# Projections whose high weight tile multiplies both parts of the activations in one product

## The chip, the core and the metric
The kernel runs on one core of a Trainium2 chip. The metric is the device time of one execution in microseconds: 2598.18 us as the median of three runs before the change. PE is TensorE, PEld its weight loads, DVE VectorE, ACT ScalarE, POOL GpSimd, SP SyncE, which issues the DMAs.

## The reference
256 tokens of 2048 features go through two layers of attention and then a block with an S5 state space mixer and an MLP; everything is modulated by vectors that come from large vector-matrix products. What matters here is that most of the arithmetic is dense projections `h @ W` of 256 tokens by 2048 rows of a float32 weight: query, key, value, gate and output projections, a GLU, and the MLP

```python
def sq_relu_mlp(h, w1, w2):
    return jnp.square(jax.nn.relu(h @ w1)) @ w2
```

All of it has to come out in float32 accuracy.

## The kernel before
A weight matrix is cut into column tiles of 128 columns by 2048 rows, 320 tiles in all, in a fixed list (`stream_init`). A tile is loaded in two halves of 128 x 1024 (SP's queue, tag `raw`, four buffers). `_split` (L118) makes two fp32r parts of each half: ScalarE casts the high part `wh` (L130), VectorE (or GpSimd) subtracts it from the raw half and leaves the low part `wl` (L131). High and low parts have five buffers each (tags H and L). Before each tile's products `weights()` makes sure that two more tiles are split ahead (`ahead = 2`) and takes one step of the side jobs: `bg()` loads a chunk of a vector product and adds the chunk before, on VectorE (L210) or on TensorE (L195), by the policy of the stage.

The activations are split in the same way into `aH` and `aL`, each `[128, 16, 256]` (`pair`, `affine_split` L392, L393). `mm_t` (L149) makes 128 output columns by 256 tokens of the next tile: 16 steps over the rows, each with three products of 256 columns,

```python
self.nc.tensor.matmul(ps, h, aH, start=kt == order[0], stop=False)   # L156
self.nc.tensor.matmul(ps, h, aL, start=False, stop=False)            # L157
self.nc.tensor.matmul(ps, l, aH, start=False, stop=kt == order[-1])  # L158
```

Each product loads its own 128 x 128 weight tile. The sum `pj` lies in PSUM in one of four banks (`NPJ = 4`). 288 tiles go through `mm_t`: 48 in layer 0's input projections and 16 in its output, 16 keys, 32 of layer 1's query and gate and 16 of its output, 32 of the GLU and 128 of the MLP. The 32 tiles of the values go through `mm_n` (L173 to L175), where the activations are the loaded operand; it is not changed.

Who reads `pj`: ScalarE copies it (keys, first quarter of the MLP's output L1588), scales it (queries; out_norm's gate, L1037), or takes tanh of it, whereupon VectorE reads it a second time (gates, GLU L1516); in the MLP ScalarE applies Relu (L1579), VectorE squares (L1581), and the square is split again; the later quarters of the MLP's output are added by VectorE (L1590). Where a projection ends a stage (out_norm, GLU, MLP) sums over its output follow on TensorE (`band`) and a chain of small VectorE instructions before the next stage starts.

The order of the instructions on each engine is made by the tile framework's scheduler from the program; each engine runs its queue in order. The forget gate's products (L1109 to L1111) use the same format with a weight tile of 16 columns; the attention's scores (L875) are float32, in two passes each.

Of the kernel before, what the change touches and what calls it, by code (L numbers as in the profile page):

```python
# [101 lines left out]
def bc(ap, n):  # L102
    """ap [p, m] seen as [p, m, n], each element repeated n times."""
    return bass.AP(tensor=ap.tensor, offset=ap.offset, ap=[list(d) for d in ap.ap] + [[0, n]])


class K:
# [11 lines left out]
    def _split(self, eng=None):  # L119
# [4 lines left out]
        for i in range(2):  # L124
            raw = self.raw.tile([128, 1024], F32, name=f"w{j}_{i}", tag="raw")
            nc.sync.dma_start(raw, self.items[j][:, i * 1024:i * 1024 + 1024])
            h = self.hl.tile([128, 8, 128], F32R, name=f"wh{j}_{i}", tag="H")
            l = self.hl.tile([128, 8, 128], F32R, name=f"wl{j}_{i}", tag="L")
# [20 lines left out]
    def mm_t(self, a, order=range(KT)):  # L149
        """[128 columns, 256 tokens] of the next column tile; a[kt] = both parts of [128, 256]."""  # L150
        H, L = self.weights()
        ps = self.pj.tile([128, T], F32, name="pj", tag="pj")
        for kt in order:
            h, l = H[kt // 8][:, kt % 8], L[kt // 8][:, kt % 8]
            aH, aL = a(kt)
            self.nc.tensor.matmul(ps, h, aH, start=kt == order[0], stop=False)  # L156
            self.nc.tensor.matmul(ps, h, aL, start=False, stop=False)  # L157
            self.nc.tensor.matmul(ps, l, aH, start=False, stop=kt == order[-1])  # L158
        return ps

    def mm_n(self, a, half):
        """[128 tokens, 2, 256 columns]: half 0 opens the sum with the first 8 kt, half 1 closes it."""
# [92 lines left out]
    def bg_add(self, *jobs):  # L255
        """Queue (name, generator): the first halves of all, then the second."""
# [4 lines left out]
    def policy(self, engines, split):  # L261
        """The engines that add the chunks, and which halves of the weights GpSimd splits."""
# [3 lines left out]
    def bg(self, n=1, eng=None):  # L266
        """n steps of the vector products: each loads a chunk and adds the one before."""
# [25 lines left out]
    def rsqrt(self, v):  # L293
        """v[128, n] (positive) -> v ** -0.5: a guess from the exponent, a step of Newton's and one of Halley's."""
# [5 lines left out]
        # y = 3/8 of the better guess  # L300
# [9 lines left out]
    def spread(self, col, name="rb"):  # L310
        """col[128 tokens, n, 2] -> PSUM [128, n, 256], the value of each token in every partition."""
# [11 lines left out]
    def colsum(self, ps, src, first, last, cols=None):  # L323
        """ps[128 tokens, 2, n] += src[128, 256].T @ cols[128, n] (cols: ones)."""
# [6 lines left out]
    def bands(self, name):  # L331
        """PSUM [128, 256] of zeros for band()."""
# [7 lines left out]
    def band(self, g, q, cols, src):  # L340
        """Rows 32 q .. of g += cols[128, n].T @ src[128, 256]."""
# [3 lines left out]
    def band_sums(self, g, sel, name):  # L345
        """PSUM [128 tokens, 2, n]: the rows of g that sel[128, n] picks and adds."""
# [20 lines left out]
    def small_bg(self, out, a, b, c, d):  # L367
        """a * (1 + b) and c * (1 + b) + d (without c: d), by halves."""
# [16 lines left out]
    def affine_split(self, src, S, B, dst, js=range(KT)):  # L385
        """dst(kt) = both parts of src(kt) * S + B."""
# [13 lines left out]
    def s5_exp(self, x, t, em1=False):  # L400
        """x, t: lists of [128, 128] scratch; returns exp(x) (or exp(x) - 1) in t[0]."""
# [19 lines left out]
    def cmul(self, o, a, b, t):  # L421
        """complex pairs: o = a * b; t: four scratch tiles."""
# [12 lines left out]
    def s5_compact(self):  # L435
# [25 lines left out]
        # w = (lambda_bar - 1) / a  # L461
# [15 lines left out]
        # powers  # L477
# [5 lines left out]
        # factors of the tables by half blocks: [hb, table (W, V), ri, 8 groups, 4 tokens]  # L483
# [17 lines left out]
        # chunk decay and its squarings, per group ((re, im), (-im, re))  # L501
# [12 lines left out]
    def s5_prod(self, t, xr, xi, lr, li, part):  # L514
        """t = the two products of part 0 (real) or 1 (imaginary) of x * l, x [128, n, 16], l [128, n, 4]."""
# [58 lines left out]
        # C A^|lag| of 4 groups by lag -3 .. 3, zero where the lag is the other direction's  # L574
# [79 lines left out]
    def chunk_inputs(self, w, Ub, q, evac):  # L654
        """w[128 (s, tau, h), 4, 2, 128 (dir, state)], Ub[128, 8, 2, 64], group pairs 4q .. 4q+3:
# [428 lines left out]
    def layer1(self):  # L1084
# [138 lines left out]
        for h in range(16):  # L1223
# [6 lines left out]
            if h:  # L1230
                pv(h - 1)
# [473 lines left out]
```

## Time and profile before

| | before |
|---|---|
| median of 3 runs (lowest, highest) | 2598.18 us (2596.72, 2598.43) |
| profiled execution: span, first to last instruction | 2600.7 us |
| instructions | 52283 |
| granted TensorE clock, mean | 0.946 |
| read from and written to HBM | 613.71 MB, 25.69 MB |

The profile is of one execution; its own time is known by its span alone. A share is the busy time of an engine over the span. Products are pipelined, so the duration of one is longer than the distance to the next; the pace is read from the starts. A granted clock of 1.00 is 2.4 GHz.

### The profile page before, as it was taken

To read this page: it belongs to the slowest core of one execution; us is meant where nothing else is said; L and a number is where in the kernel's file an instruction comes from. 1 tells how busy PE (TensorE), PEld (TensorE's weight loads), DVE (VectorE), ACT (ScalarE), POOL (GpSimd) and SP (SyncE) were. 2 spreads that over 40 slices of the span, in tenths; PEclk is the share of its full clock that TensorE was granted. 3 is DMA by queue.
4 is the path that set the end of the run, shared out by engine and by line. 5 is a ranking of instruction groups with operands and counts; after the bars stand their busy time and mean duration, and the time that the engine had idled before them with its cause. 6 is when DMAs were issued, how large, how long until landed. Compare 5 with 4: busy or idle time off the path is not lost.

```text
span 2600.7 us, 52283 instructions
## 1 busy us (share of the span) xinstructions
PE 2397.3 (92%) x20998; PEld 2172.4 (84%) x20998; DVE 1755.7 (68%) x3223; ACT 1255.6 (48%) x2178; POOL 209.7 (8%) x432
## 2 busy tenths in 40 slices
PE   5699999999899999999997445999899999999997
PEld 1299999999688888898886335998899999999996
DVE  3287878868766555788778998876754554555554
ACT  1455544444365565766555155544544443443442
POOL 0000000000011110000000853000000000000000
PEclk9699999999899999999998766999899999999998
DMA  9999999878779998788776543996355555555552
GB/s 330 343 337 318 333 329 329 317 253 326 252 248 339 333 328 289 264 279 283 258 232 204 182 165 120 331 318 238 119 184 183 184 184 182 186 180 186 182 179 94
DMA packets 203332, 644.92 MB, mean 248 GB/s; under 512 B 41009, under 2 KB 49457, under 8 KB 202705
## 3 DMA queue, kind: packets, MB, share of 16 engines
q1 hardware_dynamic: 195616, 620.47, 69.3%
q0 software_dynamic: 7472, 21.11, 2.1%
q8 instruction: 164, 2.69, 0.4%
q14 instruction: 80, 0.65, 0.1%
HBM read 613.71 MB, written 25.69 MB: 246 GB/s over the span
## 4 chain that ended last, share of the span: by engine, by line
PE 83%; DVE 10%; DMA 3%; ACT 3%; issue 1%; SPq 0%; DVEq 0%; POOL 0%; ACTq 0%
PE pj L156 22%; PE pj L157 21%; PE pj L158 21%; PE g L195 3%; DVE scan_t L1381 3%; PE pjv L173 3%; PE pjv L174 2%; DMA graw<-in_w_mod 2%; PE pjv L175 2%; DVE scan_t L1380 2%; DVE S L1382 2%; PE inc L665 1%; PE st L343 1%; PE kps L617 1%; PE ys L343 1%
## 5 line engine op out<-in xcount | busy, mean ns | idle before, releaser
L131 DVE TENSOR_TENSOR wl<-w,wh 128x1024 fp32r<-128x1024 f32 x638 | 777.6, 1224 | 533.7 <-ACT wh L130 526.0
L130 ACT CAST wh<-w 128x1024 fp32r<-128x1024 f32 x640 | 664.9, 1048 | 717.2 <-PE pj L157 414.0
L157 PE MATMUL pj<-h2L,wh 128*128 128x256 f32 x1024 | 291.1, 286 | 0.4 <-DVE h2L L393 0.3
L156 PE MATMUL pj<-h2H,wh 128*128 128x256 f32 x1024 | 286.8, 286 | 4.7 <-ACT h2H L392 3.6
L158 PE MATMUL pj<-h2H,wl 128*128 128x256 f32 x1024 | 290.7, 285 | 0.0
L156 PE MATMUL pj<-dH,wh 128*128 128x256 f32 x1024 | 290.1, 284 | 0.0
L157 PE MATMUL pj<-dL,wh 128*128 128x256 f32 x1024 | 289.9, 283 | 0.0
L158 PE MATMUL pj<-dH,wl 128*128 128x256 f32 x1024 | 289.9, 283 | 0.0
L210 DVE SCALAR_TENSOR_TENSOR gacc<-graw,csilu,gacc 128x1024 f32<-128x1024 f32 x207 | 264.7, 1279 | 26.0 <-DMA graw<-in_w_mod 16.5
L156 PE MATMUL pj<-hH,wh 128*128 128x256 f32 x768 | 221.5, 289 | 5.2 <-ACT hH L392 4.0
L158 PE MATMUL pj<-hH,wl 128*128 128x256 f32 x768 | 221.4, 289 | 0.5 <-DVE wl L131 0.5
L157 PE MATMUL pj<-hL,wh 128*128 128x256 f32 x768 | 221.1, 288 | 0.0
L195 PE MATMUL g<-graw,czc 128*32 128x256 f32 x1776 | 169.8, 466 | 51.3 <-DMA graw<-in_w_mod 49.9
L156 PEld LDWEIGHTS pj<-h2H,wh 128*128 128x128 f32 x1024 | 196.0, 194 | 5.7 <-ACT h2H L392 4.1
L157 PEld LDWEIGHTS pj<-h2L,wh 128*128 128x128 f32 x1024 | 198.6, 194 | 1.2 <-DVE h2L L393 1.2
L158 PEld LDWEIGHTS pj<-h2H,wl 128*128 128x128 f32 x1024 | 198.8, 194 | 0.1
L156 PEld LDWEIGHTS pj<-dH,wh 128*128 128x128 f32 x1024 | 196.8, 192 | 1.7 <-issue 1.7
L158 PEld LDWEIGHTS pj<-dH,wl 128*128 128x128 f32 x1024 | 196.8, 192 | 0.0
L157 PEld LDWEIGHTS pj<-dL,wh 128*128 128x128 f32 x1024 | 196.8, 192 | 0.0
L195 PEld LDWEIGHTS g<-graw,czc 128*32 128x32 f32 x1776 | 47.2, 120 | 130.5 <-DMA graw<-in_w_mod 105.5
L156 PEld LDWEIGHTS pj<-hH,wh 128*128 128x128 f32 x768 | 148.7, 194 | 8.8 <-ACT hH L392 4.1
L158 PEld LDWEIGHTS pj<-hH,wl 128*128 128x128 f32 x768 | 148.4, 193 | 4.5 <-issue 3.7
(476 smaller groups left out, 5907.6 us busy)
## 6 DMA issues: line engine op xcount, KB each, us to landing
graw<-in_w_mod SPq DMA_DIRECT2D x384, 512.0 KB, 5.7
w<-in_mlp_in SPq DMA_DIRECT2D x128, 512.0 KB, 3.5
w<-in_mlp_out SPq DMA_DIRECT2D x128, 512.0 KB, 3.6
w<-in_a_in SPq DMA_DIRECT2D x96, 512.0 KB, 5.9
graw<-in_w_kvmod SPq DMA_DIRECT2D x64, 512.0 KB, 6.0
w<-in_b_in SPq DMA_DIRECT2D x64, 512.0 KB, 5.8
w<-in_glu SPq DMA_DIRECT2D x64, 512.0 KB, 5.4
w<-in_a_v SPq DMA_DIRECT2D x32, 512.0 KB, 5.8
```

The source lines that it names most:

```text
L130: nc.scalar.copy(h, src)
L131: (eng or (nc.gpsimd if next(self.spl) else nc.vector)).tensor_sub(l, src, h)
L156: self.nc.tensor.matmul(ps, h, aH, start=kt == order[0], stop=False)
L157: self.nc.tensor.matmul(ps, h, aL, start=False, stop=False)
L158: self.nc.tensor.matmul(ps, l, aH, start=False, stop=kt == order[-1])
L173: self.nc.tensor.matmul(ps[:, i], aH[:, s], h, start=half == 0 and i == 0 and k == 0, stop=False)
L174: self.nc.tensor.matmul(ps[:, i], aH[:, s], l, start=False, stop=False)
L175: self.nc.tensor.matmul(ps[:, i], aL[:, s], h, start=False, stop=half == 1 and i == 1 and k == 7)
L195: nc.tensor.matmul(st["g"][32 * q:32 * q + 32], self.cz[c][:, ch * 2 + s], raw[s][:, q * 256:q * 256 + 256], start=st["n"] == 0, stop=ch = ...
L210: nc.vector.scalar_tensor_tensor(acc, raw[s], cc, acc, op0=MUL, op1=ADD)
L343: self.nc.tensor.matmul(g[32 * q:32 * q + n], cols, src, start=False, stop=False)
L1381: e.tensor_add(u, t[:, :, 0], s[:, :, :, c + 1])
```

## The change
`mm_t` takes a whole PSUM bank, `[128, 2, 256]`. Both parts of an activation lie next to each other, so that the high weight tile multiplies both in one product of 512 columns; the product of the low weight tile with `aH` goes to the first half. `total` then adds the two halves: ScalarE copies (or scales) the second half to SBUF, VectorE adds the first half from PSUM. The last three quarters of the MLP's output are added to the accumulator by two VectorE additions. The MLP's Relu becomes a maximum inside the square. Weight parts share one tile (tag HL, five buffers), `pair`, `oo`, `kv` and the S5 stage's buffers are laid out to match, and two `issue_after` orders behind a ScalarE copy are gone.

```diff
-            h = self.hl.tile([128, 8, 128], F32R, name=f"wh{j}_{i}", tag="H")
-            l = self.hl.tile([128, 8, 128], F32R, name=f"wl{j}_{i}", tag="L")
+            hl = self.hl.tile([128, 2, 8, 128], F32R, name=f"w{j}_{i}", tag="HL")
+            h, l = hl[:, 0], hl[:, 1]
...
-        ps = self.pj.tile([128, T], F32, name="pj", tag="pj")
+        ps = self.pj.tile([128, 2, T], F32, name="pj", tag="pj")
         for kt in order:
             h, l = H[kt // 8][:, kt % 8], L[kt // 8][:, kt % 8]
-            aH, aL = a(kt)
-            self.nc.tensor.matmul(ps, h, aH, start=kt == order[0], stop=False)
-            self.nc.tensor.matmul(ps, h, aL, start=False, stop=False)
-            self.nc.tensor.matmul(ps, l, aH, start=False, stop=kt == order[-1])
+            aH, _ = a(kt)
+            self.nc.tensor.matmul(ps, h, view(aH, 0, [[T, 2], [1, T]]), start=kt == order[0], stop=False)
+            self.nc.tensor.matmul(ps[:, 0], l, aH, start=False, stop=kt == order[-1])
         return ps
 
+    def total(self, ps, out=None, scale=1.0):
+        out = self.tmp("pt") if out is None else out
+        t = self.tmp("ps")
+        if isinstance(scale, float) and scale == 1.0:
+            self.nc.scalar.copy(t, ps[:, 1])
+            self.nc.vector.tensor_add(out, ps[:, 0], t)
+        else:
+            self.nc.scalar.mul(t, ps[:, 1], scale)
+            self.nc.vector.scalar_tensor_tensor(out, ps[:, 0], scale, t, op0=MUL, op1=ADD)
+        return out
...
     def pair(self, name):
-        H, L = self.act_tile(F32R, name + "H"), self.act_tile(F32R, name + "L")
-        return lambda kt: (H[:, kt], L[:, kt])
+        t = [self.act.tile([128, 8, 2, T], F32R, name=f"{name}{i}", tag="act") for i in range(2)]
+        return lambda kt: (t[kt // 8][:, kt % 8, 0], t[kt // 8][:, kt % 8, 1])
...
-                nc.scalar.copy(kT[:, i], ps)
+                self.total(ps, kT[:, i])
...
-                ps = self.mm_t(h_)
+                ps = self.total(self.mm_t(h_))
                 t = self.tmp("tg")
                 nc.scalar.activation(t, ps, AF.Tanh, scale=0.5)
...
-            nc.scalar.mul(yg, ps, gate[:, j:j + 1])
+            self.total(ps, yg, gate[:, j:j + 1])
...
-            with self.tc.issue_after(nc.scalar.copy(af, pa).ins):
-                nc.scalar.activation(x[:, j], x[:, j], AF.Identity, scale=V("lg1")[:, j:j + 1],
-                                     bias=V("lb1")[:, j:j + 1])
+            af = self.total(pa)
+            nc.scalar.activation(x[:, j], x[:, j], AF.Identity, scale=V("lg1")[:, j:j + 1],
+                                 bias=V("lb1")[:, j:j + 1])
...
-                ps = self.mm_t(h_)
-                r = self.tmp("r")
-                nc.scalar.activation(r, ps, AF.Relu)
+                r = self.total(self.mm_t(h_))
                 f = self.tmp("r2")
-                v.tensor_mul(f, r, r)
+                v.scalar_tensor_tensor(f, r, 0.0, r, op0=MAX, op1=MUL)
...
-                    nc.scalar.copy(acc[:, j], ps)
+                    self.total(ps, acc[:, j])
                 else:
-                    v.tensor_add(acc[:, j], acc[:, j], ps)
+                    for i in range(2):
+                        v.tensor_add(acc[:, j], acc[:, j], ps[:, i])
```

## Rows read from the trace of the kernel before

**Rows 1.** The page's busy times (share of the span) and instructions of each engine.
```profile
PE 2397.3 (92%) x20998; PEld 2172.4 (84%) x20998; DVE 1755.7 (68%) x3223; ACT 1255.6 (48%) x2178; POOL 209.7 (8%) x432
```
**Rows 2.** The page's chain that ended last, shares of the span by engine and line.
```profile
PE 83%; DVE 10%; DMA 3%; ACT 3%; issue 1%; SPq 0%; DVEq 0%; POOL 0%; ACTq 0%
PE pj L156 22%; PE pj L157 21%; PE pj L158 21%; PE g L195 3%; DVE scan_t L1381 3%; PE pjv L173 3%; PE pjv L174 2%; DMA graw<-in_w_mod 2%; PE pjv L175 2%; DVE scan_t L1380 2%; DVE S L1382 2%; PE inc L665 1%; PE st L343 1%; PE kps L617 1%; PE ys L343 1%
```
**Rows 3.** Busy time by stage; then granted clock, DMA share and GB/s.
```profile
0.00:153.00 153.00, 101.95 (x768) 47.83 (x769) 57.09 (x188) 55.20 (x131) 5.56 (x21) 0.81 0.92 330
153.00:640.00 487.00, 487.00 (x4141) 464.81 (x4141) 393.65 (x606) 240.55 (x413) 22.24 (x45) 1.00 0.90 320
640.00:750.00 110.00, 96.65 (x654) 76.67 (x653) 82.82 (x137) 51.02 (x96) 4.86 (x15) 0.84 0.70 228
750.00:1000.00 250.00, 250.00 (x2566) 217.51 (x2566) 146.24 (x212) 145.11 (x280) 42.52 (x92) 1.00 0.94 328
1000.00:1245.00 245.00, 244.26 (x2123) 218.00 (x2122) 191.99 (x333) 160.37 (x329) 4.84 (x10) 1.00 0.81 278
1245.00:1345.00 100.00, 98.00 (x856) 86.12 (x854) 77.25 (x138) 54.84 (x98) 1.56 (x5) 0.98 0.74 252
1345.00:1620.00 275.00, 167.46 (x2089) 132.00 (x2089) 249.17 (x911) 122.55 (x230) 121.97 (x236) 0.73 0.51 169
1620.00:1815.00 195.00, 195.00 (x1597) 180.58 (x1596) 143.02 (x141) 97.54 (x156) 5.81 (x9) 1.00 0.85 299
1850.00:2575.00 725.00, 724.41 (x6036) 721.76 (x6035) 371.49 (x438) 311.13 (x417) 0.00 (x0) 1.00 0.54 178
```
**Rows 4.** Waits of PE over the span: total us, times, longest us.
```profile
PE g L195 <- DMA graw<-in_w_mod: 49.9, 58, 5.5
...
PE pj L156 <- ACT wh L130: 2.9, 4, 1.2
...
PE pj L158 <- DVE wl L131: 2.0, 3, 1.2
```
**Rows 5.** Timeline of PE in the MLP, start and duration, first and 27th product.
```profile
1999.83 0.28 PE L156 MATMUL pj<-dH,wh 128*128 128x256 f32 x1
...
2002.95 0.28 PE L158 MATMUL pj<-dH,wl 128*128 128x256 f32 x1
```
**Rows 6.** Timeline of PE at the forget gate, first and last of 45 products.
```profile
737.01 0.28 PE L1109 MATMUL zf<-kH,wzH 128*16 128x256 f32 x1
...
742.09 0.28 PE L1111 MATMUL zf<-kH,wzL 128*16 128x256 f32 x1
```
**Rows 7.** Timeline of PE at a head's scores in layer 0, four passes merged.
```profile
167.98 1.03 PE L875 MATMUL sc<-attn_ws 128*128 128x256 f32 x4
168.66 0.47 PE L157 MATMUL pj<-hL,wh 128*128 128x256 f32 x1
```
**Rows 8.** Groups of PE by form: the scores' passes of 256 columns (busy us, mean ns).
```profile
L875 PE MATMUL sc<-attn_ws 128*128 128x256 f32 x32 | 8.3, 379 | 0.0
```
**Rows 9.** Groups of VectorE and ScalarE instructions that read `pj`, and the MLP's square.
```profile
L1590 DVE TENSOR_TENSOR acc<-acc,pj 128x256 f32<-128x256 f32 x47 | 19.8, 421 | 41.3 <-PE pj L158 41.3
L1588 ACT COPY acc<-pj 128x256 f32<-128x256 f32 x16 | 5.8, 365 | 0.0
L1037 ACT ACTIVATE yg<-pj,m 128x256 f32<-128x256 f32 x12 | 5.7, 471 | 1.9 <-PE pj L158 1.9
L1581 DVE TENSOR_TENSOR r<-r 128x256 f32<-128x256 f32 x64 | 26.9, 420 | 0.0
```
**Rows 10.** The page's groups: the two instructions that split a weight half.
```profile
L131 DVE TENSOR_TENSOR wl<-w,wh 128x1024 fp32r<-128x1024 f32 x638 | 777.6, 1224 | 533.7 <-ACT wh L130 526.0
L130 ACT CAST wh<-w 128x1024 fp32r<-128x1024 f32 x640 | 664.9, 1048 | 717.2 <-PE pj L157 414.0
```
**Rows 11.** Timeline of VectorE where the MLP's last tile ends.
```profile
2578.91 0.42 DVE L1590 TENSOR_TENSOR acc<-acc,pj 128x256 f32<-128x256 f32 x1 [5.33 <-PE pj L158]
```
**Rows 12.** Busy time by stretches of 50 us: the one with the highest rate.
```profile
600.00:650.00 50.00, 50.00 (x400) 44.34 (x399) 44.40 (x53) 21.06 (x31) 1.49 (x2) 1.00 0.97 361
```

More of the change, by code (lines that the diff above doesn't have):

```diff
@@ L732, in run @@
                 self.layer0()
-            with tc.tile_pool(name="kv", bufs=32) as self.kv, tc.tile_pool(name="act1", bufs=3) as self.act:
+            with tc.tile_pool(name="kv", bufs=16) as self.kv, tc.tile_pool(name="act1", bufs=3) as self.act:
                 self.layer1()
@@ L859, in layer0 @@
         m0 = self.m0
-        oo = [self.act.tile([128, 2, 8, T], F32R, name="o1", tag="act"), None]
+        oo = [self.act.tile([128, 8, 2, T], F32R, name="o1", tag="act"), None]
         gen = self.s5_inputs_table(self.act.tile([128, 4096], F32, name="gen_ws", tag="act"))
@@ L863, in layer0 @@
         h_ = self.h0
-        o_ = lambda kt: (oo[kt // 8][:, 0, kt % 8], oo[kt // 8][:, 1, kt % 8])
+        o_ = lambda kt: (oo[kt // 8][:, kt % 8, 0], oo[kt // 8][:, kt % 8, 1])
         kT, qT, v, sg, p, o = [ws[:, i * 512:(i + 1) * 512].rearrange("p (c t) -> p c t", c=2) for i in range(6)]
@@ L936, in layer0 @@
                 self.flush(gen)
-                oo[1] = self.act.tile([128, 2, 8, T], F32R, name="o2", tag="act")
+                oo[1] = self.act.tile([128, 8, 2, T], F32R, name="o2", tag="act")
                 self.policy(POL0, X_OL0)
@@ L947, in layer0 @@
                 ps = self.mm_t(h_)
-                nc.scalar.mul(qT[:, i], ps, QS)
+                self.total(ps, qT[:, i], QS)
                 if prev is not None:
@@ L1135, in forget_t @@
             nc.vector.tensor_copy(FT, fp)
-        kT, v = [], []
+        kv, kT, v = [], [], []
         self.policy(P_KV, X_KV)
@@ L1147, in layer1 @@
                 ps = self.mm_t(k_)
-                t = self.kv.tile([128, T], F32, name=f"k{j}", tag="kv")
-                with self.tc.issue_after(nc.scalar.copy(t, ps).ins):
-                    nc.scalar.activation(z[:, j], z[:, j], AF.Identity, scale=V("lg0")[:, j:j + 1],
-                                         bias=V("lb0")[:, j:j + 1])
+                kv.append(self.kv.tile([128, 2, T], F32, name=f"kv{j}", tag="kv"))
+                t = kv[j][:, 0]
+                self.total(ps, t)
+                nc.scalar.activation(z[:, j], z[:, j], AF.Identity, scale=V("lg0")[:, j:j + 1],
+                                     bias=V("lb0")[:, j:j + 1])
                 kT.append(t)
@@ L1156, in layer1 @@
                     for h in range(2):
-                        t = self.kv.tile([128, 2, 128], F32, name=f"v{j - 17 + h}", tag="kv")
+                        t = kv[j - 17 + h][:, 1].rearrange("p (i c) -> p i c", i=2)
                         nc.scalar.copy(t, ps[:, :, h * 128:h * 128 + 128])
@@ L1207, in pv @@
             nc.vector.scalar_tensor_tensor(f, ps, 0.5, sg, op0=MUL, op1=MUL)
-            aH = self.kv.tile([128, T], F32R, name=f"oH{h}", tag="kv")
-            aL = self.kv.tile([128, T], F32R, name=f"oL{h}", tag="kv")
+            t = self.kv.tile([128, 2, T], F32R, name=f"o{h}", tag="kv")
+            aH, aL = t[:, 0], t[:, 1]
             nc.scalar.copy(aH, f)
@@ L1225, in layer1 @@
             ps = self.mm_t(h_)
-            nc.scalar.mul(qT, ps, QS)
+            self.total(ps, qT, QS)
             if h:
@@ L1231, in layer1 @@
                 pv(h - 1)
+            ps = self.total(ps)
             t = self.tmp("tg1")
@@ L1356, in s5_mix @@
                 self.to_chunks(us, ub[b % 2], U[:, b], uc, k < DVE_W)
+                wq = self.hl.tile([128, 2, 4, 2, 128], F32, name="wl", tag="HL")
                 for q in range(2):
-                    w = self.hl.tile([128, 4, 2, 128], F32, name="wl", tag="HL"[q])
+                    w = wq[:, q]
                     nc.sync.dma_start(w.rearrange("p i r x -> p (i r x)"), self.d_w[2 * b + q])
@@ L1393, in within @@
         def within(b):
+            vq = self.hl.tile([128, 2, 8, 4, 2, 16], F32, name="vl", tag="HL")
             vt = []
             for q in range(2):
-                vt.append(self.hl.tile([128, 8, 4, 2, 16], F32, name="vl", tag="H"))
+                vt.append(vq[:, q])
                 nc.sync.dma_start(vt[q].rearrange("p n t r h -> p n (t r h)"), self.d_v[b, :, 8 * q:8 * q + 8])
@@ L1428, in s5_mix @@
                 nxt = within(blocks[n + 1])
+            snq = self.hl.tile([128, 2, 8, 2, 64], F32, name="sn", tag="HL")
             for q in range(2):
-                sn = self.hl.tile([128, 8, 2, 64], F32, name="sn", tag="L")
+                sn = snq[:, q]
                 g = 16 * (b - r.start) + 8 * q
@@ L1505, in s5_mix @@
             pa = self.mm_t(z_, kts)
-            af = self.tmp("ga")
-            with self.tc.issue_after(nc.scalar.copy(af, pa).ins):
-                nc.scalar.activation(x[:, j], x[:, j], AF.Identity, scale=V("lg1")[:, j:j + 1],
-                                     bias=V("lb1")[:, j:j + 1])
+            af = self.total(pa)
+            nc.scalar.activation(x[:, j], x[:, j], AF.Identity, scale=V("lg1")[:, j:j + 1],
+                                 bias=V("lb1")[:, j:j + 1])
             if j:
@@ L1513, in s5_mix @@
             nc.scalar.activation(xq, x[:, j], AF.Square)
-            pg = self.mm_t(z_, kts)
+            pg = self.total(self.mm_t(z_, kts))
             t = self.tmp("gg")
```

## The prediction
> **What bounds the kernel now.** I read the busy shares first, then the chain that ended last, then the busy time by stage, and only then single instructions. TensorE is busy for 92% of the span, and the chain lies on it for 83% of the span, 64% on the three product lines of mm_t [rows 1, 2]. By stage [rows 3] the picture splits. From 153 to 640 us (layer 0's projections), 750 to 1000 (keys and values), 1000 to 1245 (query and gate), 1620 to 1815 (GLU) and 1850 to 2575 (MLP) PE is busy but for less than a microsecond each, at the full granted clock; those stages are 1902 us of the 2600.7. In the start, at 640 to 750 and in the scans of 1345 to 1620 it is not, and a cheaper product brings nothing there. What PE does wait for is little: 49.9 us for the vector products' chunks, and only 2.0 and 2.9 us for either part of a split weight tile [rows 4]. So the time is the pace at which PE issues products, and the change is worth what it does to that pace.
>
> **That pace.** In the MLP products start every 120 ns: 26 steps from 1999.83 to 2002.95 [rows 5]. 256 columns at 2.4 GHz, the level that a granted clock of 1.00 stands for, are 106.7 ns, so 13.3 ns per product are something else. Two rows narrow it. The forget gate's products have the same format and the same 256 columns, but a weight tile only 16 wide: 44 steps in 5.08 us, 115.5 ns each [rows 6]. So 8.8 ns stay without a long weight load, and some 4.5 come with it. The attention's fp32 passes of 256 columns, whose weights are 128 wide as here, follow each other every (1.03 - 0.38) / 3 = 217 ns [rows 7, 8]: that is 512 columns' worth of the array at 2.4 GHz (213.3) plus 3.3, with the next load fully hidden.
>
> **The change, part by part.**
> *Products.* mm_t gives 288 tiles of 16 steps, 4608 steps. A step is now three products, 3 x 120 = 360 ns. It becomes one of 512 columns and one of 256. The second keeps its 120 ns, since the next weight tile still loads beside it. The first is not in the trace. From below: 217 ns, as the fp32 passes. From above: 240, for nothing in the rows makes one product dearer than the two it replaces, which stream the same columns and load the weights twice. If what is added to the stream is paid per product, it is 213.3 plus 8.8 to 13.3, or 222 to 227. I take 224, because the forget gate's row has the same format and shows most of the extra with hardly a load. That saves 16 ns per step, 4608 x 16 = 74 us; the ends are 0 and 4608 x 23 = 106 us.
>
> The Trainium skill, "TensorE: Matmul & The Clock Gate", section "Back-to-back issue gap", gives N / 2.4 + 2.5 ns for an isolated warm product. By it two products of 256 cost 218.4, one of 512 costs 215.8, and the whole change would bring 4608 x 2.6 = 12 us. The 120 ns of rows 5 against its 109.2 speaks against that for this format; the 217 of rows 7 against its 215.8 agrees.
>
> *Evictions.* Each of the 288 tiles now leaves PSUM by a ScalarE pass over one half and a VectorE pass over the other. A VectorE addition from PSUM of this size takes 421 ns, the ScalarE copy 365 and the scaled one 471 [rows 9]. In most places the ScalarE pass replaces one of the same size (the MLP's Relu becomes a copy; the maximum moves into the VectorE square, 420 ns before and, I take it, after). So VectorE gets 288 x 0.42 = 121 us more and ScalarE about 48 x 0.37 = 18 us (the gates, whose tanh now reads SBUF). None of this is on the path as long as it fits beside PE: in the MLP VectorE works 371 us of 725 and takes 128 x 0.42 = 54 more, which fits. In layer 0's projections it works 394 of 487 and takes 64 x 0.42 = 27 more, while the stage shrinks by 16: 421 of 471, or 89%. Query and gate go from 192 of 245 to 205 of 237 [rows 3]. The addition waits for ScalarE's copy, and behind it in VectorE's queue stands the next split of a weight tile (1.22 us), for which PE waits. The cover is that the split runs up to two tiles, some 11 us, ahead: ScalarE's cast waited 414 us for PE to let weight buffers go, not the other way round [rows 10].
>
> *Tails.* Where a stage's last tile is consumed, one more dependent pass stands before the next step: in the MLP VectorE's addition begins right after the last product [rows 11], and a second one follows, +0.42 us; after the GLU and the two output projections a pass and its handover, some 0.5 us each. Together 2 us lost.
>
> *DMA.* The weights do not change, so a shorter stage asks for a higher rate. Layer 0 moves 320 GB/s and the keys and values 328, at shares of 0.90 and 0.94; the start, where PE waits for chunks, shows 330, and the best 50 us show 361 [rows 3, 12]. With the gain in full layer 0 needs 320 x 487 / 471 = 331. That is at the edge. Since VectorE is also dense there, I count half of the gain of the 80 mm_t tiles of these two stages as lost: 80 x 16 x 16 ns = 20 us, of which 10. In the MLP 178 GB/s leave room.
>
> *At nothing.* Laying both parts of an activation or of a weight tile next to each other moves no work: same bytes, same number of casts and subtractions, same number of halves in the weight ring. Shared buffers of the S5 stage serve as many blocks as before. A PSUM tile is held about half a microsecond longer, with four banks and some 5.5 us per tile. The dropped orders behind a ScalarE copy only free that queue. If these covers fail, weight loads come late, which is the rival below.
>
> *Sum.* 74 - 10 - 2 = 62 us. The profiled span is 2600.7 us, 2.5 above the median of 2598.2; what lies around the span is not shown, and I take the difference off the median: 2536 us.
>
> **The rivals.**
> *A. The extra goes with the columns, not with the product.* Then 512 columns cost 2 x 115.5 = 231 ns or more, up to 240 - 3.3 = 237. For it: the only row with this format and a hidden load still is 8.8 ns above the stream, and nothing shows whether that doubles. Against it: the fp32 passes show that the array takes 512 columns' worth at 217. Gain 9 to 3.3 ns per step, 41 to 15 us, less the tails' 2 and half of the first stages' share: 2565 to 2588. The section of the Trainium skill's "TensorE: Matmul & The Clock Gate" named above, with 2.5 ns as all that is paid per product, speaks for the far end. A product that gets broken in two again would be at the end of this case, no gain, 2600; the rows of L156 would show it by their count.
> *B. VectorE becomes the bound where it is already dense.* From 153 to 640 us and 1000 to 1345 us the extra addition then pushes each split back by its 0.42 us, PE waits for the low weights, and neither stage gains. With the 16 tiles of the keys these are 64 + 16 + 32 + 16 = 128 tiles: 54 us lost, against 160 x 16 x 16 ns = 41 us gained in GLU and MLP: with the tails 2598 + 54 - 41 + 2 = 2613 us, slower. It decides once VectorE's work comes near the stage's length, and the 89% above is a mean over denser stretches. Against it: PE's waits for a split are 2.0 us in all now.
> *C. DMA holds all stages to 1000 us at today's pace.* The 80 tiles then give nothing, another 10 us: 2546 us. It is faster all the same.
>
> **How the numbers follow.** The forecast has 0.60, A 0.22, B 0.10, C 0.08. A measurement of this kernel can tell about 0.2%, 5 us, from no change. Faster by more: forecast, C and three quarters of A, 0.84; within it: the far end of A, 0.06; slower: B, 0.10. The range goes from the cheapest product, 2598 - 106 + 2 = 2494, taken as 2497, to the far end of A, 2590; B and the extreme of A are left out.
>
> **What would show it.** In the timeline of the MLP, steps of about 224 and 120 ns in turn, and 288 x 16 products at either line; the MLP stage shorter by 128 x 16 x 16 ns = 33 us, whatever the early stages do. VectorE some 121 us busier and no new wait of PE for the low weights in the waits. Rival A shows as 231 to 240 ns after a wide product; B as PE waiting for VectorE's splits before 1345 us with the MLP faster all the same; C as PE waiting for ScalarE's cast behind a DMA, with the rate near 360 GB/s. I am wrong if the wide product's step is above 231 ns, or if the MLP gains and the whole does not.

## The result, and the profile after

The changed kernel takes 2614.29 us (median of 4 runs, 2606.01 to 2620.36), beside 2598.3 for the kernel before on the same chip: a ratio of 1.0062, 95% interval [1.0042, 1.0081]. It is slower by 16 us. The forecast was 2536 us, faster, in a range that ends at 2590. The profiled execution took 2606.01 us, the least of the four. The executions also scatter more: 14 us between four runs, where the four of the kernel before scatter by 2.5 (its larger sets beside the experiments, of 7 to 17 runs, scatter by 6 to 9).

In the kernel after, the wide product is L157 and the narrow one L158; `total`'s ScalarE copy is L166, its VectorE addition L167; with a scale they are L169 and L170. First the page's busy times and its chain, as in [rows 1, 2]:

```profile
PE 2357.5 (91%) x16390; PEld 1907.5 (73%) x16390; DVE 1865.1 (72%) x3511; ACT 1277.6 (49%) x2226; POOL 221.3 (8%) x432
...
PE 79%; DVE 12%; DMA 5%; ACT 3%; issue 1%; SPq 0%; DVEq 0%; POOL 0%; ACTq 0%
```

The 4608 products fewer are there (20998 - 16390), and PE is busy for 40 us less. But PE's share of the chain fell from 83% to 79%, and VectorE's rose from 10% to 12%: PE now waits. The busy time by stage (columns as in [rows 3], the stages' edges moved to where they now lie) shows where:

```profile
153.00:640.00 487.00, 481.73 (x3259) 417.96 (x3258) 407.07 (x651) 246.10 (x425) 22.88 (x44) 1.00 0.91 320
640.00:750.00 110.00, 93.55 (x492) 65.35 (x490) 87.99 (x148) 57.65 (x109) 4.90 (x15) 0.86 0.72 234
750.00:1000.00 250.00, 242.63 (x2296) 196.16 (x2297) 150.41 (x232) 138.82 (x271) 46.02 (x92) 0.99 0.93 323
1000.00:1260.00 260.00, 245.67 (x1655) 194.55 (x1655) 197.25 (x352) 160.14 (x331) 6.01 (x8) 0.95 0.78 260
1260.00:1370.00 110.00, 102.59 (x689) 79.47 (x688) 84.07 (x154) 59.20 (x111) 5.37 (x4) 0.97 0.69 227
...
1640.00:1840.00 200.00, 200.00 (x1170) 157.34 (x1166) 157.92 (x178) 101.05 (x163) 9.61 (x10) 0.99 0.83 292
1850.00:2575.00 725.00, 715.28 (x4097) 621.10 (x4097) 455.16 (x639) 330.94 (x442) 0.00 (x0) 0.99 0.56 180
```

In the four rows from 640 to 1370 us PE is idle for 16.5 + 7.4 + 14.3 + 7.4 = 46 us; in the four of [rows 3] that answer to them it was 13.4 + 0 + 0.7 + 2.0 = 16. Another 5 us are new ahead of 640 us. The granted clock of query and gate, 1.00 before, is 0.95. The GLU (1640 to 1840) stays full, and so does the MLP (1850 to 2575) but for its first microseconds.

A few of PE's waits over the span, as in [rows 4]:

```profile
PE tp L1211 <- ACT ws L1206: 10.0, 3, 3.7
...
PE pj L157 <- issue: 5.9, 1, 5.9
...
PE pj L158 <- DVE w L131: 5.1, 5, 1.9
...
PE st L355 <- DVE xres L1040: 4.1, 2, 2.8
```

The wait for VectorE's low weights grew only from 2.0 to 5.1 us. New are the transposes of an attention head (`tp`) that wait for ScalarE's part of the softmax. The sums of out_norm (`st`) wait longer for VectorE, 4.1 us against 1.4 before. The 5.9 us for which the profile names no releaser (`issue`) lie between layer 0's output projection and the keys.

The pace in the MLP, PE's timeline as in [rows 5], six steps:

```profile
2200.09 0.39 PE L157 MATMUL pj<-d,w 128*128 128x512 f32 x1
2200.32 0.27 PE L158 MATMUL pj<-d,w 128*128 128x256 f32 x1
2200.43 0.40 PE L157 MATMUL pj<-d,w 128*128 128x512 f32 x1
...
2202.17 0.39 PE L157 MATMUL pj<-d,w 128*128 128x512 f32 x1
```

A step is 2.08 / 6 = 347 ns. On the mean of 90 tiles of the MLP the next product starts 232 ns after the wide one and 115 ns after the narrow one; the step had been 360, and the forecast was 344.

And the evictions, VectorE's and ScalarE's groups by form (busy us, mean ns), beside [rows 9]:

```profile
L166 ACT COPY ps<-pj 128x256 f32<-128x256 f32 x176 | 65.0, 372 | 188.0 <-PE pj L158 186.4 <-DVE fa L1133 1.1
L167 DVE TENSOR_TENSOR pt<-pj,ps 128x256 f32<-128x256 f32 x128 | 53.7, 420 | 55.5 <-ACT ps L166 55.1 <-POOL m L242 0.3
...
L170 DVE SCALAR_TENSOR_TENSOR yg<-pj,m,ps 128x256 f32<-128x256 f32 x32 | 15.2, 478 | 11.7 <-ACT ps L169 11.7
```

Their sizes are as forecast (the additions that also scale take 478 ns in place of 420): VectorE is busy 1865.1 - 1755.7 = 109 us more, against 121.

### The profile page after: what moved, and what is told of

Its sections match the earlier page's. It is cut to its first block, busy times and chain, and to the rows that moved or that the text cites. A ratio compares the mean times of both kernels' runs of the same rounds, so it can differ in the third digit from the quotient of the medians.

```text
span 2604.2 us, 43486 instructions
## 1 busy us (share of the span) xinstructions
PE 2357.5 (91%) x16390; PEld 1907.5 (73%) x16390; DVE 1865.1 (72%) x3511; ACT 1277.6 (49%) x2226; POOL 221.3 (8%) x432
## 4 chain that ended last, share of the span: by engine, by line
PE 79%; DVE 12%; DMA 5%; ACT 3%; issue 1%; SPq 0%; DVEq 0%; POOL 0%; ACTq 0%
PE pj L157 40%; PE pj L158 20%; DMA graw<-in_w_mod 3%; PE g L207 3%; DVE scan_t L1395 3%; PE pjv L185 2%; DVE scan_t L1396 2%; PE pjv L186 2%; DVE S L1397 2%; PE pjv L187 2%; PE inc L677 1%; PE ys L355 1%; DVE w L131 1%; ACT ub L1295 1%; DVE gacc L222 1%
## 5 line engine op out<-in xcount | busy, mean ns | idle before, releaser
L131 DVE TENSOR_TENSOR w<-w,w 128x1024 fp32r<-128x1024 f32 x638 | 778.4, 1223 | 334.3 <-ACT w L130 329.6
L130 ACT CAST w<-w 128x1024 fp32r<-128x1024 f32 x640 | 667.5, 1049 | 539.5 <-PE pj L158 409.9
L157 PE MATMUL pj<-h,w 128*128 128x512 f32 x2304 | 822.7, 400 | 12.1 <-DVE h L405 9.2
L158 PE MATMUL pj<-h,w 128*128 128x256 f32 x2304 | 651.3, 283 | 1.5 <-DVE w L131 1.5
L157 PEld LDWEIGHTS pj<-h,w 128*128 128x128 f32 x2304 | 436.2, 189 | 121.8 <-issue 10.7
L158 PEld LDWEIGHTS pj<-h,w 128*128 128x128 f32 x2304 | 438.3, 190 | 12.4 <-issue 7.0
L157 PE MATMUL pj<-d,w 128*128 128x512 f32 x1024 | 357.1, 395 | 0.0
L158 PE MATMUL pj<-d,w 128*128 128x256 f32 x1024 | 284.4, 278 | 0.0
L157 PEld LDWEIGHTS pj<-d,w 128*128 128x128 f32 x1024 | 192.1, 188 | 46.8 <-PE pj L158 1.8
L157 PE MATMUL pj<-o,w 128*128 128x512 f32 x512 | 189.8, 410 | 5.0 <-DVE yg L170 2.7
L158 PEld LDWEIGHTS pj<-d,w 128*128 128x128 f32 x1024 | 192.5, 188 | 0.0
L157 PE MATMUL pj<-z,w 128*128 128x512 f32 x512 | 186.2, 405 | 1.0 <-ACT w L130 1.0
L166 ACT COPY ps<-pj 128x256 f32<-128x256 f32 x176 | 65.0, 372 | 188.0 <-PE pj L158 186.4
L158 PE MATMUL pj<-o,w 128*128 128x256 f32 x512 | 146.9, 287 | 1.9 <-DVE w L131 1.9
L158 PE MATMUL pj<-z,w 128*128 128x256 f32 x512 | 146.1, 286 | 2.0 <-POOL w L131 2.0
L157 PEld LDWEIGHTS pj<-o,w 128*128 128x128 f32 x512 | 97.8, 191 | 38.5 <-issue 11.4
L157 PEld LDWEIGHTS pj<-z,w 128*128 128x128 f32 x512 | 97.1, 190 | 31.2 <-issue 4.3
L157 PE MATMUL pj<-k,w 128*128 128x512 f32 x256 | 100.2, 428 | 8.8 <-issue 5.9
```

What stands on the lines that cost most here:

```text
L130: nc.scalar.copy(h, src)
L131: (eng or (nc.gpsimd if next(self.spl) else nc.vector)).tensor_sub(l, src, h)
L157: self.nc.tensor.matmul(ps, h, view(aH, 0, [[T, 2], [1, T]]), start=kt == order[0], stop=False)
L158: self.nc.tensor.matmul(ps[:, 0], l, aH, start=False, stop=kt == order[-1])
L166: self.nc.scalar.copy(t, ps[:, 1])
```

## The experiments

All kernels are the changed kernel with a switch: mm_t is told its stage, and stages that are not in a list (here the full one) go the old way, in three products of 256 columns into a tile of 256, with the old evictions and orders. The layout of the change (both parts side by side, its buffers) stays everywhere.

```diff
+WIDE = ("l0", "out0", "k", "qg", "out1", "glu", "mi", "mo")   # all: the changed kernel
-    def mm_t(self, a, order=range(KT)):
+    def mm_t(self, a, st, order=range(KT)):
...
+        wide = st in WIDE
+        ps = self.pj.tile([128, 2, T] if wide else [128, T], F32, name="pj", tag="pj")
```

In these kernels the wide and the narrow product are L161 and L162, the old three L168 to L170, and `total` adds at L187 and L190.

The table has the length of each stage in us, worked out from the traces: from the last product of the stage before, for layer 0's inputs from their own first tile, to the stage's last product (the values, 122 to 125 us everywhere, start and tail are left out). "out0" and "out1" are the output projections, "k" the keys with the norm ahead of them, "qg" query and gate, "S5, GLU" everything from layer 1's norm to the GLU's end. The row below "out0 and k" is a part of it, the time from out0's last product to the keys' first. The MLP's step is a mean over at least 80 of its tiles. Runs' medians stand below; each stage is read from the one profiled execution.

| | before | layout e4 | two 256 e2 | first half e3 | idle copy e6 | after | after, again e8 | e5 | e12 |
|---|---|---|---|---|---|---|---|---|---|
| layer 0 inputs | 454.8 | 457.5 | 457.0 | 449.9 | 456.9 | 449.2 | 448.7 | 449.4 | 448.6 |
| out0 and k | 271.7 | 261.1 | 279.3 | 262.0 | 270.5 | 283.2 | 287.3 | 261.4 | 258.4 |
| of it, out0's end to k's start | 14.3 | 11.7 | 17.8 | 13.6 | 17.6 | 20.3 | 20.3 | 13.5 | 13.5 |
| qg | 278.3 | 276.3 | 279.2 | 282.2 | 280.9 | 293.2 | 292.8 | 278.4 | 278.8 |
| out1 | 133.8 | 130.0 | 137.4 | 128.4 | 131.1 | 139.8 | 142.7 | 130.4 | 130.2 |
| S5, GLU | 441.0 | 440.3 | 443.9 | 440.9 | 444.3 | 443.2 | 443.7 | 438.4 | 439.5 |
| MLP | 763.4 | 761.8 | 763.7 | 746.8 | 767.0 | 736.9 | 750.2 | 747.3 | 749.9 |
| MLP's step, ns | 360 | 360 | 360 | 353 | 360 | 347 | 353 | 353 | 353 |
| median of runs | 2598.3 | 2588.28 | 2617.59 | 2571.33 | 2610.12 | 2614.29 | 2620.17 | 2565.38 | 2559.32 |

**e1_mlp_wide: wide products in the MLP alone.**

```diff
-WIDE = ("l0", "out0", "k", "qg", "out1", "glu", "mi", "mo")
+WIDE = ("mi", "mo")
```

> The wide product and the two-engine eviction only in the MLP's 128 tiles; everywhere else three products of 256 columns and the old eviction, in the new layout of buffers. Theory 1 (the extra eviction pass makes the serial chains of the attention and norm stages late, PE then idles): those stages are as before and the MLP keeps the 27 us that it showed, 2571 us. Theory 2 (the new layout and shared buffers cost the time): the loss of some 62 us stays, 2630 us or more. Theory 3 (a faster PE merely runs into chains that were just hidden before): as theory 1 here, 2571 us.

Measured: 2576.29 us, ratio 0.9912 [0.9897, 0.9928]. Theory 2 falls; theories 1 and 3 expected the same 2571 us, and this run doesn't tell them apart. The change does bring time where its additions fit: 12 us against the layout alone (e4).

**e2_two_256: the evictions at the old pace.** The wide product is cut into two of 256 columns, one into each half; both halves are evicted and added as in the change.

```diff
-                self.nc.tensor.matmul(ps, h, view(aH, 0, [[T, 2], [1, T]]), start=first, stop=False)
+                self.nc.tensor.matmul(ps[:, 0], h, aH, start=first, stop=False)
+                self.nc.tensor.matmul(ps[:, 1], h, aL, start=False, stop=False)
```

> The changed kernel with the 512-column product cut back into two of 256 columns, each with its own weight load, into the same two halves of the bank; eviction and layout stay. Theory 1: the pace goes back by 58 us and the late chains stay, 2640 to 2672 us. Theory 2: the same, about 2660 us. Theory 3: at the old pace the chains are hidden again, 2598 to 2610 us.

Measured: 2617.59 us, ratio 1.007 [1.0055, 1.0085]: between what theories 1 and 2 expected and what theory 3 did, and as slow as the changed kernel. Against the layout alone (e4) the evictions cost 29 us, of them 18 in out0 and the keys and 7 in out1.

**e3_first_half: the wide products with the old evictions.** Only the first half of the sum is read, so the products with the low part of the activations are left out of the result, though they are made.

```diff
-        return ps
+        return ps[:, 0]
```

> The changed kernel, but only the first half of the bank is evicted, by the old single instruction; the second half, the products with the low part of the activations, is computed and left out of the result. Theory 1: the pace's gain of 58 us stays and what was given back does not occur, 2540 to 2555 us. Theory 2: as the changed kernel, about 2610 us. Theory 3: the chains are still shorter covered than before, 2580 to 2600 us.

Measured: 2571.33 us, ratio 0.9887 [0.9871, 0.9904]. That is between theory 1 and theory 3. Against e4 all wide products together bring 17 us, 3.7 ns per step where 16 were forecast; in the MLP, where nothing else changes, the step itself is 6.7 ns shorter. Query and gate even become 6 us longer.

**e4_layout: the layout alone.**

```diff
-WIDE = ("l0", "out0", "k", "qg", "out1", "glu", "mi", "mo")
+WIDE = ()
```

> The kernel before in products and evictions, with the new layout alone (both parts of weights in one buffer, both parts of activations side by side, the key and value buffers in pairs, the S5 buffers to match). Theories 1 and 3: 2595 to 2602 us. Theory 2: most of 62 us slower, 2640 us or more.

Measured: 2588.28 us, ratio 0.996 [0.9945, 0.9974], below what any theory expected. The part that was costed at nothing brings 10 us, nearly all in out0, the keys and out1. So the rest of the change costs 26 us, not 16.

**e5_l0_mlp: wide where the first runs showed a gain.**

```diff
-WIDE = ("l0", "out0", "k", "qg", "out1", "glu", "mi", "mo")
+WIDE = ("l0", "mi", "mo")
```

> Wide products and two-engine evictions in layer 0's input projections and in the MLP alone, the new layout everywhere. The layout alone ran at 2588 us; the wide MLP took 12 us off that, and layer 0's input projections were 8 us shorter with the wide product whichever eviction followed. Theory B1 (VectorE's in-order queue is held up where it is dense: the output projections, the keys, query and gate) and B2 (the handover from ScalarE to VectorE lengthens the chains there): 2565 to 2570 us. If layer 0's eight microseconds are given back in the next stage: 2574 to 2578 us.

Measured: 2565.38 us (2564.72 to 2565.83), ratio 0.9873 [0.986, 0.9885], faster than either kernel. Layer 0's gain is not given back in the next stage; B1 and B2 expected the same here.

**e6_dve_load: VectorE's pass alone.** The layout with three narrow products and old evictions, and beside them one VectorE copy of each tile from PSUM that nobody reads.

```diff
+        self.nc.vector.tensor_copy(self.tmp("idle"), ps)
         return ps
```

> The layout with the old three products and the old evictions, and one more VectorE pass per tile of mm_t: a copy of the tile from PSUM to a buffer that nobody reads. VectorE gets 288 x 0.42 us of work, no chain gets longer. Theory B1: it costs what the real evictions cost at the old pace, 2588 to about 2610 us or more. Theory B2: at most a few microseconds, 2588 to 2595 us.

Measured: 2610.12 us, ratio 1.0047 [1.0035, 1.006], 22 us over e4, as B1 expected. The copy's own view (count, shortest, median and longest ns):

```profile
L171 DVE COPY idle<-pj x288: 386/425/426, 136.7 to 2585.9; 128x256 f32<-128x256 f32 x144
```

288 instructions of 0.42 us that nothing in the result needs cost 22 us, where the evictions cost 29 in e2. But they don't cost it in the same places. In out0 and the keys it is 9 of e2's 18, of which 6 are the stretch from out0's last product to the keys' first (11.7 us in e4, 17.6 here, 17.8 in e2); in out1 only 1 of 7. Some 14 lie in query and gate, the S5 stage with the GLU, and the MLP, where e2 itself loses 8. So VectorE's work alone explains the stretch ahead of the keys; for the rest of out0, the keys and out1 the second dependent pass, or another order of the queues, is left as the reason, which no run tested by itself.

Why such a copy costs so much is seen at the end of out0, in VectorE's timeline. First the layout alone:

```profile
683.75 1.22 DVE L134 TENSOR_TENSOR w<-w,w 128x1024 fp32r<-128x1024 f32 x1
684.89 1.28 DVE L246 SCALAR_TENSOR_TENSOR gacc<-graw,csilu,gacc 128x1024 f32<-128x1024 f32 x1
686.46 0.16 DVE L1092 TENSOR_SCALAR mr<-sums 128x2 f32<-128x2 f32 x1 [0.29 <-PE sums L389]
```

and then e2, with the additions:

```profile
685.60 0.48 DVE L190 SCALAR_TENSOR_TENSOR yg<-pj,m,ps 128x256 f32<-128x256 f32 x1 [1.03 <-ACT ps L189]
686.53 1.23 DVE L134 TENSOR_TENSOR w<-w,w 128x1024 fp32r<-128x1024 f32 x1 [0.45 <-ACT w L133]
687.67 1.28 DVE L246 SCALAR_TENSOR_TENSOR gacc<-graw,csilu,gacc 128x1024 f32<-128x1024 f32 x1
688.87 0.42 DVE L1074 SCALAR_TENSOR_TENSOR xres<-xres,yg 128x256 f32<-128x256 f32 x1
689.20 1.28 DVE L246 SCALAR_TENSOR_TENSOR gacc<-graw,csilu,gacc 128x1024 f32<-128x1024 f32 x1
...
690.73 2.60 DVE L246 SCALAR_TENSOR_TENSOR gacc<-graw,csilu,gacc 128x1024 f32<-128x1024 f32 x2
694.42 0.16 DVE L1092 TENSOR_SCALAR mr<-sums 128x2 f32<-128x2 f32 x1 [1.09 <-PE sums L389]
```

VectorE's queue holds the vector products' chunks (1.28 us each), the splits (1.22) and the residual (0.42) in one order. With the additions it is still working off chunks after the last projection tile, and the norm's first instruction, for which the keys wait, starts at 694.42 in place of 686.46: 9.4 us after out0's last product in place of 5.2 (8.4 with the idle copy of e6). The order in which these stand in the queue is made anew by the scheduler for every kernel, and no run held it fixed.

**e7_pool_add: the addition on GpSimd.** ScalarE copies both halves, GpSimd adds them.

```diff
-            self.nc.scalar.copy(t, ps[:, 1])
-            self.nc.vector.tensor_add(out, ps[:, 0], t)
...
+        for i in range(2):
+            self.nc.scalar.mul(t[i], ps[:, i], scale)
+        self.nc.gpsimd.tensor_add(out, t[0], t[1])
```

> The changed kernel with another eviction: ScalarE copies both halves to SBUF in two passes and GpSimd adds them (0.73 us for this size in the S5 stage), so VectorE gets nothing more except in the MLP's last three quarters, but the chain is longer by 0.6 us. Theory B1: what was lost comes back, 2570 to 2590 us. Theory B2: the longer chain costs more, 2615 to 2650 us.

Measured: 2606.44 us, ratio 1.0029 [1.0018, 1.004], between the two theories. GpSimd's groups by form (busy us, mean ns) give the price of the addition there:

```profile
L187 POOL TENSOR_TENSOR pt<-ps,pu 128x256 f32<-128x256 f32 x112 | 106.5, 951 | 898.4 <-ACT pu L186 757.2 <-PE pj L162 65.6 <-issue 44.6
L187 POOL TENSOR_TENSOR yg<-ps,pu 128x256 f32<-128x256 f32 x32 | 34.8, 1090 | 178.4 <-ACT pu L186 164.7 <-issue 6.1 <-DVE ctx_ws L1342 4.8
```

Out0, relieved of VectorE's pass, falls from 119.5 to 112.1 us; query and gate rise from 293.2 to 303.1, which fits the longer chain of ScalarE and GpSimd in a head's way, though nothing shows that chain to be the cause.

**e8_again: the changed kernel once more, in more runs.**

> The changed kernel once more, with its own profile. In the first profile a step of the MLP took 232 + 116 ns, with the same code in two experiments 236 + 117. If the pace differs from execution to execution, this one's MLP stage lies between 720 and 732 us and the times scatter over some 12 us again, 2604 to 2622; if it hangs on where the program puts its buffers, the steps are 232 + 116 again and the MLP stage is 720 us.

Measured: 2620.17 us (2603.87 to 2622.21, 6 runs), ratio 1.0068 [1.0046, 1.0091]. PE's timeline in the MLP of this execution, first and last of eight steps:

```profile
2199.63 0.40 PE L161 MATMUL pj<-d,w 128*128 128x512 f32 x1
2199.87 0.28 PE L162 MATMUL pj<-d,w 128*128 128x256 f32 x1
...
2202.47 0.40 PE L161 MATMUL pj<-d,w 128*128 128x512 f32 x1
```

2.84 / 8 = 355 ns per step here (353 on the mean of 90 tiles, 236 of them after the wide product), against 347 in the first profile, at a granted clock of 1.00 between 1900 and 2550 us in both. The MLP takes 750.2 us against 736.9; the two profiled executions are 16 us apart. The times scatter as expected for a pace that differs from execution to execution. The kernel here is not quite the same program (a temporary of the GLU has a buffer of its own), so these two profiles alone leave the place of the buffers open. The profile of e7 goes further: within its one execution, at a granted clock of 1.00, the MLP's step is 347 ns from 1886 to 1953 us, 353 from 1964 to 2133, 347 from 2145 to 2311 and 353 from 2322 to 2492.

**e9_384: what the extra goes with.** Wide products in the MLP alone, and there of 384 columns; only the first half of the sum is evicted, as in e3.

```diff
-                self.nc.tensor.matmul(ps, h, view(aH, 0, [[T, 2], [1, T]]), start=first, stop=False)
+                self.nc.tensor.matmul(view(ps, 0, [[1, 384]]), h, view(aH, 0, [[1, 384]]), start=first, stop=False)
```

> Wide products in the MLP only, and there of 384 columns in place of 512 (the last half of the low activations is left out), with only the first half of the sum evicted, so the products with the low activations part are left out of the MLP's result. If the extra goes with the columns: a step of 174 to 178 ns after the 384-column product (1.5 times 116 to 118) beside 116 to 118 after the narrow one. If it is paid once per product: 160 ns of array time plus 9 to 11, 169 to 171. If a wide product is taken in pieces of 256 columns, each with its own extra: 117 and 64, 181 or more. The MLP stage then takes 2048 steps of 290 to 294 ns, about 600 us, and the whole about 2455.

Measured: 2453.65 us in one run. PE's timeline in the MLP, the first and the last of eleven steps:

```profile
2099.75 0.34 PE L161 MATMUL pj<-d,w 128*128 128x384 f32 x1
2099.92 0.28 PE L162 MATMUL pj<-d,w 128*128 128x256 f32 x1
2100.04 0.34 PE L161 MATMUL pj<-d,w 128*128 128x384 f32 x1
...
2102.97 0.34 PE L161 MATMUL pj<-d,w 128*128 128x384 f32 x1
```

A step is 3.22 / 11 = 293 ns, on the mean of 90 tiles 176 after the wide product and 117 after the narrow one. Per column that is 0.46 ns in both, and 0.45 to 0.46 at 512 columns (232 and 236). Paid once per product it would have been 169 to 171, in pieces of 256 columns 181 or more. The extra goes with the columns.

**e10_qg: query and gate alone wide.**

```diff
-WIDE = ("l0", "out0", "k", "qg", "out1", "glu", "mi", "mo")
+WIDE = ("qg",)
```

> Layout of the change, wide products and additions in query and gate alone. If that stage loses by itself (VectorE's additions between its other work, and transposes of PE that wait for them): the stage is 288 to 294 us against 276 with the layout alone, and the whole 2598 to 2606. If its loss in the changed kernel is only the backlog that earlier stages hand on: the stage gains up to 4 us, and the whole is 2584 to 2588.

Measured: 2590.59 us, ratio 0.997 [0.9957, 0.9983]; the stage takes 282.5 us against 276.3. It loses by itself, but only 6 of the 17 us that it loses in the changed kernel: neither expectation holds. The rest appears only where the other stages are wide too. What differs is on record: the changed kernel's transposes wait 10.0 us for ScalarE in this stage, here 1.7. Why is taken up below, under *Where a pace gain went*.

**e11_out0_k: layer 0's output projection and the keys alone wide.**

```diff
-WIDE = ("l0", "out0", "k", "qg", "out1", "glu", "mi", "mo")
+WIDE = ("out0", "k")
```

> Layout of the change, wide products and additions in layer 0's output projection and the keys alone. If VectorE's queue delays TensorE there: output projection and keys together 279 to 287 us against 261 with the layout alone, and the whole 2604 to 2614. If the additions hide: up to 4 us gained, the whole 2584 to 2588.

Measured: 2600.86 us, ratio 1.0012 [1.0003, 1.0021], 13 us over e4; both stages together take 278.6 us against 261.1, almost what e2 showed. The median lies 3 us below what was expected; the sign is right.

**e12_l0_glu_mlp: the GLU wide as well.**

```diff
-WIDE = ("l0", "out0", "k", "qg", "out1", "glu", "mi", "mo")
+WIDE = ("l0", "glu", "mi", "mo")
```

> As the version with wide products in layer 0's inputs and the MLP (2565.4 us), and the GLU as well. If the GLU's additions hide and its pace gains 4 to 8 ns per step: 2 to 4 us less, 2561 to 2563. If they cost as much as they bring, as its stage in the changed kernel (443 us with the S5 part against 440) suggests: 2565 to 2569.

Measured: 2559.32 us (2554.36 to 2564.12), ratio 0.9842 [0.9822, 0.9862]. Its page:

```profile
PE 2357.2 (92%) x17670; PEld 1977.3 (77%) x17670; DVE 1836.5 (72%) x3431; ACT 1273.2 (50%) x2210; POOL 213.9 (8%) x432
```

As much PE time as the changed kernel (2357.5), without its idle time. This is the best version, 39 us below the kernel before. The 6 us beyond e5 are more than was expected, and that the GLU brings them isn't shown: its stage (439.5 us) is no shorter than in e5 (438.4). Its four runs stand in two pairs, 2554.4 and 2554.8 us, 2563.9 and 2564.1; the profiled one is of the slower pair, which lies within 2 us of e5. A faster pace of the MLP in the other pair would explain that, but it has no profile.

## Why the prediction was wrong

*What bounds the kernel* was read rightly: the time is PE's pace in its full stages, and PE's products were the place to gain. Two terms of the sum failed, the products' size and the evictions at nothing; two smaller ones, the layout and the tails, had the wrong size too.

*Products, 74 us: the step "if what is added to the stream is paid per product".* It is paid per column (e9). The wide product takes 232 ns in the first profile's MLP and 236 in that of e8, not 224: rival A, whose prices 231 and 237 bracket it. The forget gate's row [rows 6] said 115.5 ns for 256 columns with hardly a load, and twice that is the 231; I preferred the fp32 passes [rows 7] as evidence that the array takes 512 columns' worth in 217 ns, but those are another format, and their pace doesn't carry over to fp32r. The Trainium skill, "TensorE: Matmul & The Clock Gate", section "Back-to-back issue gap", gives 215.8 ns for an isolated warm product of 512 columns; the trace doesn't agree, here by 16 to 21. In the MLP the gain was 26 us in one execution and 13 in another, against 33 forecast; with the old evictions all 288 tiles gained 17 us (e4 to e3).

*Evictions "at nothing".* This is what turned the sign: +29 us at the old pace (e2). VectorE's work alone, without a longer chain, costs 22 (e6), though only in part in the same places. The step that failed is "none of this is on the path as long as it fits beside PE". The cover that I named, weight splits two tiles ahead, held: the wait for low weights is 5.1 us. But I asked only who waits for the splits. VectorE's queue also holds what no prefetch covers, the norm between out0 and the keys and the residual behind each projection tile; pushed back behind the additions, these hold PE: from out0's last product to the keys' first it is 20.3 us, before 14.3, in e4 11.7. Rival B had the engine and the queue, and its 2613 us is near the median, but not by its reasons: it wanted waits for low weights and a loss of 0.42 us per tile in layer 0's inputs, and these, with VectorE busy 407 of 487 us, gained 8 us against e4. A dense engine alone didn't decide; a chain on it that the next stage waits for did.

*Where a pace gain went.* In query and gate the wide product brings a loss instead, 6 us alone (e3) and 17 with its evictions. PE reaches the transposes of a head before ScalarE has the softmax ready. PE's timeline after the change has three such waits in the stage; the longest two (start, duration, and in brackets the idle time and its releaser):

```profile
1098.94 1.09 PE L1211 MATMUL tp<-idn,ws 128*128 128x128 f32 x3 [3.68 <-ACT ws L1206]
...
1193.15 1.08 PE L1211 MATMUL tp<-idn,ws 128*128 128x128 f32 x3 [3.69 <-ACT ws L1206]
```

In both ScalarE is not short of work of its own. Its timeline ahead of the first one, between the softmax's exponential (L1201) and its scaling (L1206):

```profile
1094.80 0.19 ACT L1201 ACTIVATION_READ_ACCUMULATOR ws<-ws,mx 128x1 f32 x1
1094.89 3.57 ACT L1295 ACTIVATE ub<-uctx,ctx_ws 64x64 f32<-64x64 f32 x8
1098.48 0.80 ACT L1206 ACTIVATE ws<-ws,sr 128x128 f32<-128x128 f32 x2
```

Eight steps of a side job (`ctx_states`, tile `ub`) fill the 3.68 us for which PE waits; ahead of the second wait it is eight again, ahead of the third, of 2.6 us, nine. In e4 no head has more than four there, nor in e10. So where the scheduler puts the side job in ScalarE's queue belongs to this loss. It isn't all of it: e2 has seven such steps in one head without that wait. No run held the order fixed.

The busy time by stretches of 10 us around the two waits (columns as in [rows 3]):

```profile
1095.00:1105.00 10.00, 5.75 (x22) 3.68 (x18) 6.68 (x20) 6.39 (x15) 0.00 (x0) 0.60 0.72 231
1105.00:1115.00 10.00, 10.00 (x71) 8.12 (x70) 6.56 (x13) 6.36 (x17) 0.84 (x2) 0.89 0.33 107
...
1185.00:1195.00 10.00, 5.74 (x52) 4.28 (x51) 7.83 (x23) 8.37 (x23) 2.34 (x2) 0.88 0.71 225
1195.00:1205.00 10.00, 10.00 (x47) 6.95 (x48) 5.50 (x14) 4.12 (x13) 0.00 (x0) 0.61 0.52 175
```

With each wait the granted clock falls (1.00 is 2.4 GHz; a value between 0.50 and 1.00 is a mean of 1.2 and 2.4 GHz): in the last row PE is busy all 10 us at 0.61, so that some 4 us of work at full clock are lost after the wait is over. For the whole stage, after the change and in e4:

```profile
968.90:1262.10 293.20, 278.87 (x1871) 218.97 (x1869) 216.71 (x383) 180.29 (x371) 8.04 (x12) 0.96 0.79 263
955.00:1231.30 276.30, 275.11 (x2437) 243.52 (x2437) 204.35 (x356) 179.72 (x370) 8.25 (x18) 1.00 0.82 283
```

PE is idle for 14.3 us in place of 1.2 (the waits for `tp` are 10.0 of it, those for `pv` 2.1), and busy for 3.8 us more although its 512 steps are some 9 ns shorter each: 13.1 + 3.8 is the 17 us by which the stage is longer. In e3, with the old evictions, the stage was already 6 us longer, so part of it is the wide product alone.

The parts do not add: -17 (e3) and +29 (e2) on e4's 2588 would be 2600, and the changed kernel is at 2614 to 2620. The table puts the 14 to 20 us in query and gate (+8), in out0 and the keys (+3 to 7) and in out1 (+4 to 7). That a gain in pace and a late VectorE make the same wait longer, so that PE spends waiting what it saves, would explain it; no run shows it apart from the order of the queues. The profiled execution of the changed kernel is nearer to 2600, since its MLP had the faster pace.

*The layout "at nothing"* was -10 us. Which of its buffers brings it in out0, the keys and out1 wasn't tried.

*The DMA's 10 us* weren't there: layer 0's inputs gained 8.3 us against e4, 10.8 ns per step, which is the pace itself (360 - 349), and PE's wait for the cast is 3.4 us against 2.9. Rival C fell. *The tails, 2 us*, were too small: the MLP's is 22.9 us against 22.1, where 0.42 was forecast, and the one between out0 and the keys, forecast at some 0.5 us, is the 6 us (against before) of the evictions' account.

Of the signs named beforehand two came: the wide product's step above 231 ns (232 and 236), and an MLP that gains where the whole doesn't.

## What to carry to other kernels

An eviction pass was not free where something on the engine's in-order queue was awaited behind it. Before costing one at nothing, look at each stage's end for the chain that stands in the same queue, not at the share of busy time or at the prefetched work alone. A saving in pace is worth taking stage by stage: here it paid in layer 0's inputs and in the MLP (-23 us on the layout), and cost time in query and gate, where heads wait for ScalarE behind a side job, and behind the output projections. Layer 0's inputs hold attention heads too, without such a wait, so it isn't the heads as such. A changed kernel also gets its queues in a new order: look there before a lost gain is put down to the change itself. Price a longer product from rows of the same number format, and test a second length before taking what is added to the stream as paid per product.

## What the runs showed of the hardware

An fp32r product with 128 x 128 weights costs 0.45 to 0.47 ns per column at 256, 384 and 512 columns, so 232 or 236 ns for 512; an fp32 pass of 256 columns takes 217 [rows 7]. The pace of the wide product has two values at the same granted clock, and can change between them within one execution (e7). On the mean of many tiles the MLP's steps are 346.7 and 353.3 ns with 512 columns, 293.3 with 384 and 360.0 with three products of 256: 52, 53, 44 and 54 times 6.67 ns. The MLP with three narrow products took 761.8 to 763.7 us before, in e4 and in e2. What decides between the two values no row shows. An addition of 128 x 256 from SBUF takes GpSimd 0.95 to 1.09 us, VectorE 0.42 even with one operand in PSUM.
